# The first norm of a two-block transformer kernel: sums of squares and scales moved from VectorE to TensorE

## The chip, the core and the metric

The kernel runs on one core of a Trainium2 chip. The metric is the device time of one execution in microseconds (us), and lower is better. The core's engines work side by side and wait for each other on semaphores: TensorE (PE, with its weight loads shown as PEld), VectorE (DVE), ScalarE (ACT), GpSimd (POOL) and SyncE (SP), which here issues DMA transfers.

## The reference, cut to what matters

Two networks of two layers run one behind the other on 512 tokens of width 1024. The change touches only the head of the first layer of the first one:

```
cond = silu(c)                                   # 1024 numbers
mod  = cond @ ada_w[0] + ada_b[0]                # 6 x 1024: sh1, sc1, g1, sh2, sc2, g2
h    = x * rsqrt(mean(x*x) + EPS) * (1 + sc1) + sh1
q, k, v, g = split(h @ w_in)                     # retention: four heads of 256
q, k = rotary(q, pos), rotary(k, pos)            # products with cos and sin of an angle
...
```

So the first projection needs x, its mean square for each token, and the 1024 scales and shifts that come out of two matrix-vector products with 1024x1024 pieces of `ada_w`.

## The kernel before

**Layout.** x lies transposed, as eight tiles `xs.x[k]` of 128 channels x 512 tokens. Every fp32 matrix product is made of three matmuls of 128x512 on halves in fp32r: h is split into `hh` and `hl`, a weight tile `raw` into `whi` (ACT, L290) and `wlo` (DVE or POOL, L291), and `mm3` (L296 to L298) issues high by high, high by low and low by high into one PSUM bank `mm`. `load_w` loads a weight tile of 128x1024 through a ring of three `raw` buffers on SP's queue. Engines take their instructions in program order, and a scheduler with priorities (`tc.high_priority`) writes that order when the kernel is built, so an instruction stands behind whatever was put ahead of it on its engine.

**The first norm.** ACT squares the eight tiles of x (L374). DVE adds the squares into `acc` (L376). Then PE multiplies the four 128-column pieces of `acc` by a column of 1/1024 (`sums`, L343): four fp32 matmuls, which the trace shows as eight passes (x8). DVE makes the inverse root in some ten instructions on 128x4 (L322 to L337), and PE spreads it over the partitions with four transposing matmuls (L351).

**The modulation.** `ada_tile` multiplies a tile of `ada_w` (`araw`, three buffers) by `cond`, held alike on all partitions, and sums along the row on DVE (L583, traced as a long and a short instruction), which gives 128 of the 6144 numbers; a tiny addition of the bias follows (L587 or L589). For the first norm 16 tiles are needed, eight scales and eight shifts, in the order scale 0, shift 0, scale 1, ... The other tiles come later, loaded by POOL.

**The normed tiles.** `mod_steps` with the order "late" makes x·R on DVE for two tiles and on POOL for six. ACT applies scale and shift (L421) and rounds to `hh` (L422). POOL subtracts for `hl` (L426). Other norms of the kernel take another branch: `t = x·scale·R` on DVE (L431), `hh = t + shift` on ACT (L433), `hl = t + shift - hh` on DVE (L434).

**Behind it.** `retention` begins with the rotary angle: one integer tile is turned into `cosT` and `sinT` by eight single DVE instructions and three on ACT (L745 to L757). Its first projection makes q and k of head 0 in four PSUM banks (`proj` with four weight tiles). DVE multiplies the four banks by `cosT` and `sinT` (L763 to L766), which frees them. The value projection follows, and then the first score matmul, `mm<-q,q`.

Of the kernel before, what the change touches and what calls it, by code (L numbers as in the profile page):

```python
# [13 lines left out]
F32 = mybir.dt.float32  # L14
# [3 lines left out]
ALU = mybir.AluOpType  # L18
# [84 lines left out]
def _host(i):  # L103
    f32 = np.float32
    h = {}
    h["xT"] = i["x"][0].T.reshape(KT, P, L)
    h["ctxT"] = i["ctx_2"][0].T.reshape(KT, P, LC)
    h["pos"] = np.broadcast_to(i["pos"], (P, L))
    for n, a in (("c1", i["c"]), ("c2", i["c_2"]), ("cc", i["c_ctx_2"])):
# [76 lines left out]
def net_kernel(ctx: ExitStack, tc: tile.TileContext, a: dict, out: bass.AP, dbg=None, stop_at=None):  # L186
# [22 lines left out]
    def tmp(w=L):  # L209
        return tp.tile([P, L], F32, tag="t", name=nm("t"), bufs=TBUFS)[:, :w]  # L210
# [70 lines left out]

    def load_w(src, n=1024):
        wp, _, bufs = next(W["raw"])
# [3 lines left out]
        lo = wp.tile([P, 1024], F32R, tag="wlo", name=nm("wlo"))  # L287
        with tc.high_priority(offset=AHEAD):
            nc.sync.dma_start(raw[:, :n], src)
            S.copy(hi[:, :n], raw[:, :n])  # L290
            next(W["low"]).tensor_tensor(lo[:, :n], raw[:, :n], hi[:, :n].bitcast(F32), ALU.subtract)  # L291
# [14 lines left out]
    def proj(srcs, h, n):  # L306


        w = [load_w(s) for s in srcs]
        p = [mm_ps()[:, :n] for _ in srcs]  # L310
# [93 lines left out]
    def mod_steps(st, R, sc, sh, res, order=None, ext=None):  # L404
# [3 lines left out]
        for k in range(KT):  # L408
            hi, lo = htile(st, k)
            if order == "late":  # L410

                if k == 0:
                    ts = [tmp(n) for _ in range(3)]
                    V.tensor_mul(ts[0], st.x[0], R)
                    V.tensor_mul(ts[1], st.x[1], R)
                    Rs = tmp(n)
                    S.copy(Rs, R)
                    G.tensor_tensor(ts[2], st.x[2], Rs, ALU.mult)
                    yield
                t = ts[k]  # L420
                S.activation(t, t, AF.Identity, bias=sh[:, k:k + 1], scale=sc[:, k:k + 1])  # L421
                S.copy(hi, t)  # L422
                if k + 3 < KT:
                    ts.append(tmp(n))
                    G.tensor_tensor(ts[k + 3], st.x[k + 3], Rs, ALU.mult)
                G.tensor_tensor(lo, t, hi.bitcast(F32), ALU.subtract)  # L426
                res.append((hi, lo))
                yield
                continue
            t = tmp(n)  # L430
# [308 lines left out]

    def retention(st, h, g1, hook, then):  # L740
        with pool("ret") as rp:
# [42 lines left out]

            p = proj(qsrc(0, 0) + qsrc(0, 1), h, L)
            qq, kk_ = rotated(0, p[:2]), rotated(1, p[2:])
# [922 lines left out]
    with ExitStack() as blk:  # L1709
# [3 lines left out]
        open_ada(adas)  # L1713
        first = [t for k in range(8) for t in (8 + k, k)]
        plan = ada_plan([(0, ["1"], first + list(range(16, 48))), (1, ["1"], range(48))])
        hs = {}
        ns = norm_steps(xs, mv("1", 0, 1), mv("1", 0, 0), hs, "late")
        with tc.high_priority(offset=2000):
            for k in range(KT):
                nc.sync.dma_start(xs.x[k], a["xT"][k])  # L1720
            take(ns, 1)
            cond("1", "c1")
            nc.sync.dma_start(pk, a["pack"])
            take(plan, 1)
            take(ns, 1)
            take(plan, 1)
            take(ns, 1)
        for k in range(1, KT):
            with tc.high_priority(offset=500) if k < 3 else nullcontext():
                take(plan, 2)  # L1730
            take(ns, 1)
        take(ns, 9)
        h = hs["x"]
        mid0 = HalfNorm(xs, mv("1", 0, 4), mv("1", 0, 3))
# [8 lines left out]

        retention(xs, h, mv("1", 0, 2), hook_r, mid0)
        if dump("x_mix0"):
# [104 lines left out]
```

## Time and profile before

| | us |
|---|---|
| three runs: median (lowest to highest) | 2926.98 (2925.31 to 2928.30) |
| the profiled execution: its time | 2927.78 |
| the profiled execution: its span in the trace | 2925.9 |
| PE busy in that span | 2833.4 |
| PE busy in 86.20 to 130.00 (43.80) | 43.75 |
| first projection matmul starts | 23.08 |
| first score matmul starts | 86.20 |

The trace is that of the profiled execution; its times count from the start of the span. Its own time is 0.80 us above the median. The granted TensorE clock is given as a share of 2.4 GHz, so 0.50 is the lower of its two levels, 1.2 GHz. In the first 41 us the column shows 1.00 while the spacing of the matmuls is that of the lower level: no clock event is recorded before the first change.

### The profile page before, as it was taken

How to read it: one execution, taken by the hardware profiler on the slowest of the kernel's cores; microseconds unless marked ns; L12 is line 12 of the kernel's file. 1: busy time of each engine (PE TensorE's matmuls, PEld its weight loads, DVE VectorE, ACT ScalarE, POOL GpSimd, SP SyncE). 2: the span in 40 equal slices, each digit the busy share in tenths (PEclk: the TensorE clock that was granted, in tenths of full speed). 3: DMA queues.
4: the chain of work that ended last, by engine and by line, in shares of the span. 5: the costliest groups of instructions: out<-in, count | busy, mean ns of one | idle time of the engine just before them, and what ended most of it. 6: DMA issues, size and time to landing. Idle time of an engine off the chain costs nothing.

```text
span 2925.9 us, 40551 instructions
## 1 busy us (share of the span) xinstructions
PE 2833.4 (97%) x15700; PEld 2382.5 (81%) x15700; DVE 1938.6 (66%) x3558; ACT 1141.8 (39%) x1865; POOL 622.6 (21%) x590
## 2 busy tenths in 40 slices
PE   5999999999998999999999999999999999999999
PEld 3888888878886887888788888888887777788887
DVE  8767667986877668898736678554348467653333
ACT  4433344323753443223434431312237477542331
POOL 4000003443323113332002022221101233022220
PEclk9999999999999999999999999999999999999999
DMA  7445433665655435555212246331214322232232
GB/s 268 136 155 168 158 119 109 221 219 171 219 197 198 150 96 179 174 179 161 76 60 98 72 125 214 112 126 51 70 54 151 100 73 74 65 101 94 91 103 73
DMA packets 122608, 384.77 MB, mean 132 GB/s; under 512 B 13232, under 2 KB 27184, under 8 KB 121392
## 3 DMA queue, kind: packets, MB, share of 16 engines
q1 hardware_dynamic: 97072, 289.90, 30.5%
q0 software_dynamic: 25344, 92.29, 9.9%
q8 instruction: 123, 2.02, 0.3%
q14 instruction: 69, 0.57, 0.1%
HBM read 359.06 MB, written 23.07 MB: 131 GB/s over the span
## 4 chain that ended last, share of the span: by engine, by line
PE 55%; DVE 9%; ACT 2%; issue 1%; POOL 0%; ACTq 0%; DVEq 0%; POOLq 0%
PE mm L296 17%; PE mm L297 17%; PE mm L298 17%; DVE aout L583 1%; DVE wlo L291 1%; DVE al L280 1%; DVE araw L583 1%; PE aux L1637 1%; PE mm L1604 1%; PE mm L1624 1%; DVE t L618 1%; ACT whi L290 1%; PE mm L1432 0%; DVE hl L434 0%; ACT ah L279 0%
## 5 line engine op out<-in xcount | busy, mean ns | idle before, releaser
L296 PE MATMUL mm<-hh,whi 128*128 128x512 f32 (+1 forms) x2872 | 1039.5, 365 | 12.9 <-ACT whi L290 6.2
L297 PE MATMUL mm<-hl,whi 128*128 128x512 f32 (+1 forms) x2872 | 1033.0, 360 | 16.0 <-POOL hl L426 13.6
L298 PE MATMUL mm<-hh,wlo 128*128 128x512 f32 (+1 forms) x2872 | 1031.9, 360 | 0.9 <-DVE wlo L291 0.8
L290 ACT CAST whi<-raw 128x1024 fp32r<-128x1024 f32 (+3 forms) x448 | 447.1, 1002 | 857.4 <-PE mm L297 722.1
L297 PEld LDWEIGHTS mm<-hl,whi 128*128 128x128 f32 x2872 | 545.0, 190 | 98.9 <-POOL hl L426 15.7
L296 PEld LDWEIGHTS mm<-hh,whi 128*128 128x128 f32 x2872 | 542.5, 190 | 101.7 <-issue 7.8
L298 PEld LDWEIGHTS mm<-hh,wlo 128*128 128x128 f32 x2872 | 544.8, 190 | 81.8 <-DVE wlo L291 1.6
L291 DVE TENSOR_TENSOR wlo<-raw,whi 128x1024 fp32r<-128x1024 f32 (+4 forms) x316 | 374.0, 1186 | 216.5 <-ACT whi L290 200.6
L291 POOL TENSOR_TENSOR wlo<-raw,whi 128x1024 fp32r<-128x1024 f32 (+3 forms) x132 | 309.4, 2345 | 915.3 <-ACT whi L290 771.5
L297 PE MATMUL mm<-al,whi 128*128 128x512 f32 (+1 forms) x898 | 330.1, 368 | 3.5 <-DVE al L280 3.5
L296 PE MATMUL mm<-ah,whi 128*128 128x512 f32 (+1 forms) x898 | 329.4, 367 | 2.6 <-ACT ah L279 2.6
L298 PE MATMUL mm<-ah,wlo 128*128 128x512 f32 (+1 forms) x898 | 328.9, 366 | 0.0
L583 DVE CUSTOM_DVE_ANT_0 araw<-araw,cond 128x1024 f32<-128x1024 f32 x192 | 249.0, 1298 | 12.2 <-DMA araw<-in_ada 11.8
L618 DVE SCALAR_TENSOR_TENSOR t<-mm,pk,t 128x511 f32<-128x511 f32 (+5 forms) x286 | 161.0, 581 | 134.9 <-ACT t L620 131.5
L579 POOL DMA_DIRECT2D araw<-in_ada x176 | 96.0, 546 | 658.6 <-DVE mod L583 264.2
L297 PEld LDWEIGHTS mm<-al,whi 128*128 128x128 f32 x898 | 170.6, 190 | 31.2 <-DVE al L280 4.6
L296 PEld LDWEIGHTS mm<-ah,whi 128*128 128x128 f32 x898 | 170.6, 190 | 30.4 <-ACT ah L279 3.0
L298 PEld LDWEIGHTS mm<-ah,wlo 128*128 128x128 f32 x898 | 170.5, 190 | 27.4
L710 DVE SCALAR_TENSOR_TENSOR x<-mm,mod,x 128x512 f32<-128x512 f32 (+1 forms) x115 | 84.2, 733 | 141.4 <-PE mm L298 141.3
L642 ACT ACTIVATE t<-t 128x512 f32<-128x512 f32 x110 | 64.6, 588 | 268.5 <-DVE t L618 250.0
L643 DVE TENSOR_TENSOR t<-mm,t 128x512 f32<-128x512 f32 x110 | 69.9, 636 | 149.8 <-PE mm L298 111.4
L280 DVE TENSOR_TENSOR al<-t,ah 128x512 fp32r<-128x512 f32 x110 | 121.7, 1107 | 41.5 <-ACT ah L279 41.3
(360 smaller groups left out, 3442.4 us busy)
## 6 DMA issues: line engine op xcount, KB each, us to landing
araw<-in_ada POOLq DMA_DIRECT2D x176, 512.0 KB, 4.2
raw<-in_up SPq DMA_DIRECT2D x176, 512.0 KB, 3.6
raw<-in_dn SPq DMA_DIRECT2D x32, 448.0 KB, 3.3
raw<-in_dn SPq DMA_DIRECT2D x32, 384.0 KB, 3.1
raw<-in_qk SPq DMA_DIRECT2D x24, 512.0 KB, 3.6
raw<-in_dn SPq DMA_DIRECT2D x32, 320.0 KB, 2.9
araw<-in_ada SPq DMA_DIRECT2D x16, 512.0 KB, 4.5
raw<-in_rqk SPq DMA_DIRECT2D x16, 512.0 KB, 4.5
```

Of the source, the lines that this page charges most:

```text
L280: eng.tensor_tensor(lo, full, hi.bitcast(F32), ALU.subtract)
L290: S.copy(hi[:, :n], raw[:, :n])
L291: next(W["low"]).tensor_tensor(lo[:, :n], raw[:, :n], hi[:, :n].bitcast(F32), ALU.subtract)
L296: T.matmul(o, lhsT=lh[0], rhs=rh[0], start=first, stop=False)
L297: T.matmul(o, lhsT=lh[0], rhs=rh[1], start=False, stop=False)
L298: T.matmul(o, lhsT=lh[1], rhs=rh[0], start=False, stop=last)
L579: (nc.sync if l == 0 and f < 16 else G).dma_start(raw, a[f"ada{l}"][f])
L583: tc.keep_in_program_order(V.tensor_tensor_reduce(out=o, in0=raw, in1=A[c], scale=1.0, scalar=0.0, op0=ALU.mult, op1=ALU.add, accum_out=m))
L618: V.scalar_tensor_tensor(to, fr, cw[q], to, ALU.mult, ALU.add)
L642: S.activation(t, t, AF.Silu)
L643: V.tensor_mul(t, pv, t)
L710: V.scalar_tensor_tensor(xv, p, gates[st.tag][:, f:f + 1], xv, ALU.mult, ALU.add)
```

## The change

**Squares.** ACT squares each tile of x into a tile of its own. PE multiplies every one of the 32 pieces of 128x128 by the column `inv` and accumulates over the eight tiles in PSUM (L1712). The seven additions on DVE and `sums` are gone here.

**Scales.** A transposed copy of the scale part of `ada_w` (`adas`) is a new input. For each k, `scale(k)` loads 128x1024 of it into one of five buffers `aw` of a pool of their own and PE multiplies its eight pieces by the columns of `cT` (c as 128x8, through ACT's Silu) into one column of the bank `pa` (L1719). One tiny DVE instruction adds 1 and the bias (L1720). The shifts stay with `ada_tile` on DVE.

**Normed tiles.** The "late" branch is deleted, and the first norm goes the way of the others: DVE, ACT, DVE (after: L413, L415, L416). ACT, which before changed its function table for Silu, loads it first.

**Loads.** SP's queue now runs: c1T, the eight tiles of x, `pack`, `aw` 0, cond, `araw` 0, two weight tiles, `aw` 1, `araw` 1, two weight tiles, then `aw` and `araw` by turns. The fourth weight tile waits for a `raw` buffer that the low half of the first one frees. The four weight tiles are handed to `retention` as `w0`.

```diff
-    def load_w(src, n=1024):
+    def load_w(src, n=1024, ahead=AHEAD):
...
-        with tc.high_priority(offset=AHEAD):
+        with tc.high_priority(offset=ahead) if ahead else nullcontext():
...
-        w = [load_w(s) for s in srcs]
+        w = [s if isinstance(s, tuple) else load_w(s) for s in srcs]
...
-            if order == "late":
...
-                t = ts[k]
-                S.activation(t, t, AF.Identity, bias=sh[:, k:k + 1], scale=sc[:, k:k + 1])
-                S.copy(hi, t)
-                if k + 3 < KT:
-                    ts.append(tmp(n))
-                    G.tensor_tensor(ts[k + 3], st.x[k + 3], Rs, ALU.mult)
-                G.tensor_tensor(lo, t, hi.bitcast(F32), ALU.subtract)
...
-            p = proj(qsrc(0, 0) + qsrc(0, 1), h, L)
+            p = proj(w0, h, L)
...
-        first = [t for k in range(8) for t in (8 + k, k)]
-        plan = ada_plan([(0, ["1"], first + list(range(16, 48))), (1, ["1"], range(48))])
+        plan = ada_plan([(0, ["1"], range(16, 48)), (1, ["1"], range(48))])
...
+            cT = small(8)
+            nc.sync.dma_start(cT, a["c1T"])
             for k in range(KT):
                 nc.sync.dma_start(xs.x[k], a["xT"][k])
-            take(ns, 1)
+            nc.sync.dma_start(pk, a["pack"])
+            S.activation(cT, cT, AF.Silu)
+            p = aux_ps()
+            for k in range(KT):
+                sq = tmp()
+                S.activation(sq, xs.x[k], AF.Square)
+                for tb in range(4):
+                    T.matmul(p[:, tb:tb + 1], lhsT=sq[:, tb * P:(tb + 1) * P], rhs=inv[:, 0:1], start=k == 0 and tb == 0, stop=k == KT - 1 and tb == 3)
+            pa = mm_ps()
+
+            def scale(k):
+                aw = stp.tile([P, D], F32, tag="aw", name=nm("aw"), bufs=5)
+                nc.sync.dma_start(aw, a["adas"][k])
+                for kk in range(KT):
+                    T.matmul(pa[:, k:k + 1], lhsT=aw[:, kk * P:(kk + 1) * P], rhs=cT[:, kk:kk + 1], start=kk == 0, stop=kk == KT - 1)
+                V.scalar_tensor_tensor(mods["1", 0][:, 8 + k:9 + k], pa[:, k:k + 1], 1.0, par("adab0", 8 + k), ALU.add, ALU.add)
+
+            scale(0)
             cond("1", "c1")
...
+            ada_tile(0, ["1"], 0)
+            with tc.high_priority(offset=60):
+                R = spread(rsqrt_s(p[:, :4], 4), 4)
+            res, w0 = [], []
+            steps = mod_steps(xs, R, mv("1", 0, 1), mv("1", 0, 0), res)
+            for k in range(KT):
+                if k:
+                    scale(k)
+                    ada_tile(0, ["1"], k)
+                if k < 2:
+                    w0 += [load_w(a["rqk"][8 * k + i], ahead=0) for i in range(2)]
+                take(steps, 1)
```

What the scheduler makes of it on two engines follows; a number behind a tile's name tells one buffer from the next.

On PE, these are the first rows of the program before: the four matmuls of the sum, the spread, and the first two normed tiles against the first weight tile.

```order
L343 MATMUL aux_170<-inv,acc_139 128x1 x4
L351 MATMUL aux_193<-ident,sm_177 128x128 x4
L296 MATMUL mm_355<-hh_198,whi_332 128x512
L297 MATMUL mm_355<-hl_199,whi_332 128x512
L298 MATMUL mm_355<-hh_198,wlo_333 128x512
L296 MATMUL mm_355<-hh_229,whi_332 128x512
L297 MATMUL mm_355<-hl_230,whi_332 128x512
L298 MATMUL mm_355<-hh_229,wlo_333 128x512
```

After, the head of the same queue, from the last of the eight groups of sums on (`t_189` is the last square, `aux_228` the spread root, `mm_195` the bank of the scales, `mm_430` and `mm_431` the first two banks of the projection):

```order
L1712 MATMUL aux_146<-inv,t_189 128x1 x4
L353 MATMUL aux_228<-ident,sm_216 128x128 x4
L1719 MATMUL mm_195<-sm_134,aw_196 128x1 x8
L298 MATMUL mm_430<-hh_245,whi_234 128x512
L299 MATMUL mm_430<-hl_246,whi_234 128x512
L300 MATMUL mm_430<-hh_245,wlo_235 128x512
L298 MATMUL mm_431<-hh_245,whi_240 128x512
L1719 MATMUL mm_195<-sm_134,aw_251 128x1 x8
L299 MATMUL mm_431<-hl_246,whi_240 128x512
L300 MATMUL mm_431<-hh_245,wlo_241 128x512
L298 MATMUL mm_430<-hh_278,whi_234 128x512
```

The one scale group that a step needs now stands between the projection's matmuls, behind the normed tile before it.

On DVE, this is a stretch in the middle of the first norm before: angle steps on `cosT` and `t_317` stand between the reductions of the modulation.

```order
L750 TENSOR_SCALAR cosT<-cosT 128x512
L587 TENSOR_TENSOR mod_74<-mod_74,pk 128x1
L752 SCALAR_TENSOR_TENSOR t_317<-cosT,t_317 128x512
L583 ISA araw_266,mod_74<-araw_266,cond_162 128x1024
L583 ISA mod_74 128x1
L752 SCALAR_TENSOR_TENSOR t_317<-cosT,t_317 128x512
L589 SCALAR_TENSOR_TENSOR mod_74<-mod_74,pk 128x1
L583 ISA araw_270,mod_74<-araw_270,cond_162 128x1024
L583 ISA mod_74 128x1
L752 SCALAR_TENSOR_TENSOR t_317<-cosT,t_317 128x512
```

After, the reduction of the last shift (`araw_400`) and what follows it at the end of the norm (`t_416` is the angle, `hl_405` the last low half of h, `wlo_574` and `wlo_608` low halves of value weights, `araw_602` a tile of the gate `g1`):

```order
L565 ISA araw_400,mod_74<-araw_400,cond_207 128x1024
L565 ISA mod_74 128x1
L569 TENSOR_TENSOR mod_74<-mod_74,pk 128x1
L728 CAST t_416<-t_414 128x512
L293 TENSOR_TENSOR wlo_574<-raw_572,whi_573 128x1024
L416 SCALAR_TENSOR_TENSOR hl_405<-t_406,mod_74,hh_404 128x512
L729 TENSOR_SCALAR t_416<-t_416,pk 128x512
L565 ISA araw_602,mod_74<-araw_602,cond_207 128x1024
L565 ISA mod_74 128x1
L732 TENSOR_SCALAR cosT<-t_416 128x512
L293 TENSOR_TENSOR wlo_608<-raw_606,whi_607 128x1024
L733 TENSOR_SCALAR cosT<-cosT 128x512
```

And a few rows further down, to the first two rotation products, which read the projection's first bank:

```order
L293 TENSOR_TENSOR wlo_794<-raw_792,whi_793 128x1024
L736 TENSOR_SCALAR t_416<-t_416 128x512
L569 TENSOR_TENSOR mod_74<-mod_74,pk 128x1
L565 ISA araw_670,mod_74<-araw_670,cond_207 128x1024
L565 ISA mod_74 128x1
L565 ISA araw_704,mod_74<-araw_704,cond_207 128x1024
L565 ISA mod_74 128x1
L746 TENSOR_TENSOR t_530<-mm_430,cosT 128x512
L747 TENSOR_TENSOR t_532<-mm_430,sinT 128x512
```

The eight angle instructions moved from between the first reductions to behind the last one, where they share the queue with five low halves of weights and four reductions of the next part; the rotation products stand behind all of them, as they stood behind them before.

## Rows read from the trace of the kernel before

**Rows 1.** The page of before: its span and the engines' busy time.

```profile
span 2925.9 us, 40551 instructions
PE 2833.4 (97%) x15700; PEld 2382.5 (81%) x15700; DVE 1938.6 (66%) x3558; ACT 1141.8 (39%) x1865; POOL 622.6 (21%) x590
```

**Rows 2.** Windows: start:end, length, busy of PE, PEld, DVE, ACT, POOL, PEclk, DMA, GB/s.

```profile
0.00:37.70 37.70, 5.37 (x16) 3.62 (x16) 27.40 (x43) 17.27 (x22) 18.44 (x20) 1.00 0.75 268
...
41.00:45.00 4.00, 4.00 (x19) 3.29 (x18) 3.93 (x10) 1.44 (x2) 1.50 (x1) 1.00 0.73 226
...
64.00:86.20 22.20, 21.97 (x96) 17.70 (x96) 21.61 (x37) 11.87 (x18) 2.15 (x4) 1.00 0.52 175
86.20:130.00 43.80, 43.75 (x220) 37.27 (x219) 26.80 (x51) 17.92 (x32) 1.06 (x2) 1.00 0.43 140
```

**Rows 3.** Timeline of PE and PEld, 0 to 40 us: start, busy time, instruction.

```profile
12.01 1.78 PEld L343 LDWEIGHTS aux<-inv,acc 128*128 128x128 f32 x8 [12.01 <-issue]
12.04 1.84 PE L343 MATMUL aux<-inv,acc 128*128 128x1 f32 x8 [12.04 <-DVE acc L376]
...
16.00 1.09 PE L351 MATMUL aux<-ident,sm 128*128 128x128 f32 x4 [2.13 <-DVE sm L335]
23.08 0.80 PE L296 MATMUL mm<-hh,whi 128*128 128x512 f32 x1 [5.98 <-ACT whi L290]
...
37.72 0.80 PE L297 MATMUL mm<-hl,whi 128*128 128x512 f32 x1 [5.04 <-POOL hl L426]
...
39.17 0.63 PE L297 MATMUL mm<-hl,whi 128*128 128x512 f32 x1
39.60 0.63 PE L298 MATMUL mm<-hh,wlo 128*128 128x512 f32 x1
```

**Rows 4.** Timeline of DVE, 0 to 43 us.

```profile
13.92 0.16 DVE L322 TENSOR_SCALAR sm<-aux 128x4 f32<-128x4 f32 x1 [2.02 <-PE aux L343]
...
15.82 1.22 DVE L583 CUSTOM_DVE_ANT_0 araw<-araw,cond 128x1024 f32<-128x1024 f32 x1
...
42.30 0.42 DVE L745 CAST t<-t 128x512 f32<-128x512 int32 x1
```

**Rows 5.** Lines by form: count, ns min/median/max, first and last start, shapes.

```profile
L431 DVE SCALAR_TENSOR_TENSOR t<-x,mod,aux x16: 725/739/747, 1643.5 to 2258.8; 128x512 f32<-128x512 f32 x16
L433 ACT ACTIVATE hh<-t,mod x24: 702/725/1323, 1456.3 to 2259.6; 128x512 fp32r<-128x512 f32 x24
```

**Rows 6.** Lines by form, 0 to 80 us: the two halves of a weight tile.

```profile
L290 ACT CAST whi<-raw x11: 1028/1046/1054, 22.0 to 75.6; 128x1024 fp32r<-128x1024 f32 x11
L291 DVE TENSOR_TENSOR wlo<-raw,whi x9: 1211/1216/2207, 24.2 to 77.6; 128x1024 fp32r<-128x1024 f32 x9
```

**Rows 7.** Timeline of SP and ACT; a DMA issue with KB and us to landing.

```profile
0.74 3.71 SPq L1720 DMA_DIRECT2D x<-in_xT  x8
...
3.56 0.63 ACT L374 ACTIVATE acc<-x 128x512 f32<-128x512 f32 x1 [1.54 <-DMA x<-in_xT]
...
6.56 3.90 ACT L374 ACTIVATE t<-x 128x512 f32<-128x512 f32 x6 [1.60 <-DMA x<-in_xT]
...
raw<-in_rqk SPq DMA_DIRECT2D x4, 512.0 KB, 6.4
```

**Rows 8.** Timeline of PE at the next sum of squares.

```profile
108.64 0.95 PE L343 MATMUL aux<-inv,acc 128*128 128x1 f32 x8
```

**Rows 9.** Timeline of PE at the first score matmul.

```profile
85.97 0.39 PE L298 MATMUL mm<-whi,hl 128*128 128x512 f32 x1
86.20 0.39 PE L296 MATMUL mm<-q,q 128*128 128x512 f32 x1
```

**Rows 10.** Windows of three later stretches, columns as in group 2.

```profile
450.55:453.96 3.41, 1.76 (x13) 1.59 (x13) 2.81 (x7) 0.90 (x3) 0.00 (x0) 1.00 0.55 162
453.96:457.37 3.41, 3.15 (x15) 2.72 (x14) 3.41 (x17) 2.00 (x5) 0.00 (x0) 0.50 0.60 195
884.04:887.45 3.41, 3.41 (x14) 3.22 (x15) 0.87 (x1) 0.00 (x0) 1.19 (x2) 0.50 0.39 115
```

More of the change, by code (lines that the diff above doesn't have):

```diff
@@ L107, in _host @@
     h["ctxT"] = i["ctx_2"][0].T.reshape(KT, P, LC)
+    h["c1T"] = i["c"].reshape(KT, P).T
+    h["adas"] = _wt(i["ada_w"][0][:, D:2 * D])
     h["pos"] = np.broadcast_to(i["pos"], (P, L))
@@ L409, in mod_steps @@
             hi, lo = htile(st, k)
-            if order == "late":
[L412 to L419, printed above, removed]
-                t = ts[k]
-                S.activation(t, t, AF.Identity, bias=sh[:, k:k + 1], scale=sc[:, k:k + 1])
-                S.copy(hi, t)
-                if k + 3 < KT:
-                    ts.append(tmp(n))
-                    G.tensor_tensor(ts[k + 3], st.x[k + 3], Rs, ALU.mult)
-                G.tensor_tensor(lo, t, hi.bitcast(F32), ALU.subtract)
-                res.append((hi, lo))
-                yield
-                continue
             t = tmp(n)
@@ L737, in ffn, with retention @@
                 j0 += nk
-    def retention(st, h, g1, hook, then):
+    def retention(st, h, w0, g1, hook, then):
         with pool("ret") as rp:
@@ L1713, in net_kernel @@
         open_ada(adas)
-        first = [t for k in range(8) for t in (8 + k, k)]
-        plan = ada_plan([(0, ["1"], first + list(range(16, 48))), (1, ["1"], range(48))])
+        plan = ada_plan([(0, ["1"], range(16, 48)), (1, ["1"], range(48))])
         hs = {}
-        ns = norm_steps(xs, mv("1", 0, 1), mv("1", 0, 0), hs, "late")
-        with tc.high_priority(offset=2000):
+        with pool("start") as stp:
+            cT = small(8)
+            nc.sync.dma_start(cT, a["c1T"])
             for k in range(KT):
@@ L1720, in net_kernel @@
                 nc.sync.dma_start(xs.x[k], a["xT"][k])
-            take(ns, 1)
-            cond("1", "c1")
[L1723 to L1733, printed above, removed]
+            nc.sync.dma_start(pk, a["pack"])
@@ L1734, in net_kernel @@
+            h = res
         mid0 = HalfNorm(xs, mv("1", 0, 4), mv("1", 0, 3))
@@ L1742, in hook_r @@
                     s5_params()
-        retention(xs, h, mv("1", 0, 2), hook_r, mid0)
+        retention(xs, h, w0, mv("1", 0, 2), hook_r, mid0)
         if dump("x_mix0"):
```

## The prediction, made before the changed kernel ran

> **What bounds the kernel now.** I read the page first: PE is busy for 97% of the span [rows 1], so the end moves when PE's queue moves. Then the windows, stage by stage. Up to 37.70 us PE is busy for 5.37 us only, while DVE has 27.40; from 86.20 to 130.00 it is busy for 43.75 of 43.80 [rows 2]. So the head of the kernel is where PE waits, and from the first score matmul, which starts at 86.20 [rows 9], it waits for almost nothing. The two programs give PE the same instructions in the same order from that matmul on. I therefore take its start as a milestone: what it moves by, the end moves by.
>
> The timelines show what the head waits for. PE's sum of squares starts at 12.04, when DVE has added the last square, and the spread of the root ends at 16.00 + 1.09 = 17.09. The first projection matmul starts at 23.08, and PE runs without gaps from 37.72, when POOL delivers the second low half [rows 3]. Of 192 matmuls of 128x512 ahead of the milestone 188 lie behind 37.72, and they fill the 48.5 us up to it nearly without a break: 21.97 of 22.20 us are busy from 64.00 [rows 2]. The clock is at its lower level at first: two matmuls start 39.60 - 39.17 = 0.43 us apart [rows 3]; from 41 on 19 fit into 4.00 us [rows 2], and at the milestone the spacing is 86.20 - 85.97 = 0.23 us [rows 9].
>
> **Unit prices.** A one-column pass on PE at the lower level: eight take 1.84 us [rows 3]. A matmul of 0.63 is followed by the next after 0.43, so 0.20 of each last one is drain, and a pass costs (1.84 - 0.20) / 8 = 0.205. At the higher level eight take 0.95 [rows 8], with a drain of 0.39 - 0.23 = 0.16 [rows 9]: 0.10 a pass. A group of eight matmuls 128x1 in fp32 is 16 passes, since four gave x8: 16 x 0.205 + 0.2 = 3.5 us at the lower level, 1.75 at the higher. What sets the pass is its weight load: PEld needs 1.78 for eight [rows 3], 0.22 each. The Trainium skill (TensorE: Matmul & The Clock Gate, section LDWEIGHTS) puts a load at columns / 1.2 ns, so 107 ns for 128 columns; by that the 64 passes of the squares would be done in 6.9 us instead of 13.1, under the arrival of x. The row measures twice that on the same shape at this level, and I go by the row.
>
> DVE: a product of t or low half of h 0.74, ACT's high half 0.73 [rows 5]; a weight's high half 1.05, its low half 1.22 [rows 6]; a shift's reduction 1.22, a tiny instruction 0.16, a step with one operand 0.42 [rows 4]. These are the durations without POOL beside it; the low half also shows 2.21 [rows 6], the upper bound for the long ones.
>
> **The change, step by step.**
>
> *Squares.* SP issues one load more ahead of x, 3.71 / 8 = 0.46 us; the first square then starts at 3.56 + 0.46 = 4.02 and ends at 4.65, the last ends at 6.56 + 3.90 + 0.46 = 10.92 [rows 7]. PE needs 64 passes: 4.75 + 64 x 0.205 + 0.2 = 18.1. The seven additions on DVE go, but PE now ends the sum, 4.2 us later than before (12.04 + 1.84 = 13.88 [rows 3]). The root and the spread are unchanged, 17.09 - 13.88 = 3.2: 21.3.
>
> *First scale.* It stands behind the spread on PE: 21.3 + 3.5 = 24.8. Its tile was issued about 5 us into the span and needs some 6 to land (6.4 for a weight of the same size [rows 7]), so it is there. Then, one behind the other, the tiny DVE instruction 0.16, t 0.74, on DVE the shift's reduction with its two tiny ones 1.22 + 0.32, and the high half 0.73: 3.2, so 28.0. ACT rounds the first weight behind that, 1.05: the first projection matmul starts at about 29 (before 23.08). The low half of this weight is ready at about 30.3.
>
> *Second scale.* It stands behind four projection matmuls, 31 to 34.6, and the same 3.2 follow: dense work from about 38, as before (37.72). What POOL's low halves cost before, two groups on PE and the later sum cost now.
>
> *Scales in the dense stretch.* Before, PE met nothing but projection matmuls here. Now six more groups stand among them. Eleven matmuls at 0.43 lead to 42.7, with the clock up by then as before; scale 2 ends at 44.8, seven matmuls and scale 3 later it is 48.1. Each further step holds one group 1.75, twelve matmuls 12 x 0.23 = 2.76 and a wait: the low half of this step comes on DVE behind the tiny one and the next t, 0.16 + 0.74 + 0.74 + 0.1 for the handover = 1.75 after the group's end, and only six matmuls, 1.36, stand between. So 0.4 is open, and a step is 4.9. Four of them: scale 7 ends at 67.7.
>
> *The end of the norm on DVE.* The rotation products, which free the bank that the third value bank needs, stand behind all of this on DVE: five low halves of weights (6.1), five reductions (6.1), six products (4.4), five steps with one operand (2.1), two rotation products (about 1.4 by the price of t): 20.1 us from the end of scale 7, so 87.8. PE itself, with 72 matmuls (16.5) from 67.7, would be there at 84.2, so it idles for 3.6 us. Before, the angle was being worked out from 42.30 [rows 4], under POOL's slow start; that cover is gone.
>
> *Sum.* From 87.8 there are 48 matmuls to the milestone, 11.0: 98.8 instead of 86.20, +12.6. On the profiled execution's 2927.78 that is 2940.4; this execution is 0.8 above the median of 2926.98, so **2940**.
>
> *What I price at nothing.* SP: its queue stands at the fourth weight tile until the first low half is done at 30.3, and the scales 2 to 7 wait behind. That weight lands at about 37; at the 268 GB/s of the first stretch [rows 2] each further 512 KB takes 2 us, a scale with its shift 4, against 4.9 us a step. Scale 2 would be there at 39, needed at 42.7. The cover is 4 us; if the rate were a third lower, each later step would lose about 1 us, 5 in all. One load of ACT's function table less: under the loads of x. POOL: it has nothing in the norm now, and nobody waits for it.
>
> **The rivals.**
>
> *The clock stays or falls low in the norm.* Each step has a group of one-column passes and a wait. After a stretch with PE busy 1.76 of 3.41 us the clock was at 0.50 in the next [rows 10]. At the lower level a step costs 1.75 + 12 x 0.2 - 0.4 = 3.8 more. One or two such steps give 2944 to 2948, all to the end of the norm 2955 or so. Against it: from 64.00 to 130.00 the level held at 1.00 [rows 2].
>
> *The clock comes up in the squares.* PE is now busy without a break from 4.75 on. If the clock rose some 4 us in, as it did behind 37.72, 45 of the passes would cost 0.10, and the sum ends at 13.2 (-4.9). Two groups of 1.75 (-3.5) and the first eleven matmuls at 0.23 (-2.2) follow: +12.6 - 10.6 = +2, so 2929, no change that this kernel's measurement can tell (0.2%, 5.9 us, either way). The Trainium skill (TensorE: Matmul & The Clock Gate, Part 1) says that sustained matmul activity releases the clock, and by that page this is what would happen. Against it speaks 884.04 to 887.45: PE is busy there for all of 3.41 us, and the clock is 0.50 [rows 10]. So a busy PE has been seen at the lower level.
>
> *Faster.* It takes the clock of the last case and an end of the norm in which DVE is not late: -3.6 more is 2926, still no change. To pass 2921 the dense stretch must begin before 26 and lose nothing behind: PE's own work from there is 188 x 0.23 + 6 x 1.75 = 53.7, so a milestone below 80. It decides at the sum of squares, which would have to end near the last square, 10.9.
>
> **Chances and range.** The forecast 0.58, on its own 2934 to 2947: DVE's long instructions at 2.21 would add 5, loads 5, and the late low halves may cost less (up to -6 if DVE is ready with PE and the steps have no wait). Clock low 0.20. Clock up early 0.16, of which a part falls between. Faster 0.06. The range 2928 to 2952 leaves out the faster case and the worst of the low clock. Slower 0.78, same 0.16, faster 0.06.
>
> **What would show it.** L1712 as a row of about 64 passes that ends near 18, not 11; the first projection matmul near 29 and the gapless stretch from 38; the groups of L1719 at 3.5 and later 1.75 us; the last shift's reduction near 69 and a wait of PE for DVE's rotation products (releaser t, from the first bank) just ahead of the milestone, which starts near 99; equal spacing behind it. I am wrong if passes in the squares run at 0.10, if scale 2 waits for a DMA, or if the milestone moves and the end doesn't.

## The result: 0.5% slower, and the profile after

The changed kernel takes 2941.56 us (median of five, 2940.41 to 2950.56) against 2927.20 (2925.31 to 2930.08). The ratio is 1.0052 with an interval of 1.0040 to 1.0064. The prediction was 2940. The profiled execution took 2941.22, 13.4 more than that of before.

The span on the page of the kernel after, beside [rows 1]:

```profile
span 2939.4 us, 40867 instructions
```

TensorE's timeline after, up to the third scale, beside [rows 3]:

```profile
4.99 13.79 PE L1712 MATMUL aux<-inv,t 128*128 128x1 f32 x64 [4.99 <-ACT t L1710]
20.91 1.08 PE L353 MATMUL aux<-ident,sm 128*128 128x128 f32 x4 [2.13 <-DVE sm L337]
21.79 3.41 PE L1719 MATMUL mm<-sm,aw 128*128 128x1 f32 x16
29.26 0.80 PE L298 MATMUL mm<-hh,whi 128*128 128x512 f32 x1 [4.06 <-ACT whi L292]
...
31.54 3.41 PE L1719 MATMUL mm<-sm,aw 128*128 128x1 f32 x16
...
38.07 1.22 PE L298 MATMUL mm<-hh,whi 128*128 128x512 f32 x2 [2.06 <-ACT hh L415]
...
42.42 1.84 PE L1719 MATMUL mm<-sm,aw 128*128 128x1 f32 x16
```

The first row is the squares: 64 passes in 13.79 us, from the first square on; they end at 18.78, not 13.88. The first scale ends at 25.20, the second stands among matmuls at 31.54, gapless work begins at 38.07. At 42.42 the third group takes 1.84 us, so the clock has risen by then.

And further on, to the first score matmul (beside [rows 9]):

```profile
65.96 1.84 PE L1719 MATMUL mm<-sm,aw 128*128 128x1 f32 x16
...
84.82 0.39 PE L300 MATMUL mm<-whi,hl 128*128 128x512 f32 x1
87.40 0.50 PE L298 MATMUL mm<-whi,hh 128*128 128x512 f32 x1 [2.19 <-DVE t L747]
...
98.41 0.39 PE L298 MATMUL mm<-q,q 128*128 128x512 f32 x1
```

The last scale's group ends at 67.80. The row of 87.40 shows a wait of 2.19 us for VectorE's second rotation product. The milestone is at 98.41, 12.2 later than before.

VectorE's timeline at the end of the norm:

```profile
67.84 0.16 DVE L1720 SCALAR_TENSOR_TENSOR mod<-mm,pk 128x1 f32<-128x1 f32 x1 [2.09 <-PE mm L1719]
...
70.70 0.42 DVE L728 CAST t<-t 128x512 f32<-128x512 int32 x1
...
82.23 1.23 DVE L293 TENSOR_TENSOR wlo<-raw,whi 128x1024 fp32r<-128x1024 f32 x1 [0.55 <-ACT whi L292]
...
86.06 0.69 DVE L746 TENSOR_TENSOR t<-mm,cosT 128x512 f32<-128x512 f32 x1
86.67 0.68 DVE L747 TENSOR_TENSOR t<-mm,sinT 128x512 f32<-128x512 f32 x1
```

Between the last scale (67.84) and the product that frees the bank (86.67) it has one gap only, of 0.55 us for ScalarE's high half of a weight. The rest is reductions, low halves and, from 70.70 on, the angle.

The waits of TensorE in 0 to 100 us, after (engine and line that waited, who released it, total, times, longest):

```profile
PE aux L1712 <- ACT t L1710: 5.0, 1, 5.0
PE mm L298 <- ACT whi L292: 4.1, 1, 4.1
PE mm L298 <- DVE t L747: 2.2, 1, 2.2
PE aux L353 <- DVE sm L337: 2.1, 1, 2.1
PE mm L298 <- ACT hh L415: 2.1, 1, 2.1
PE mm L299 <- DVE hl L416: 1.4, 5, 0.7
```

No load of a scale is among them, and nothing waits for GpSimd any more.

The next sum of squares starts 12.2 us later too (120.79, before 108.64 [rows 8]). Further on the shift changes, for the most part where one of the two kernels has a stretch at the lower clock and the other has none. From the sum at 463.48 (before 452.82) to that at 2220.18 (before 2209.64) it is 10.5 to 11.1 us: in 443.00 to 449.00 the kernel before was granted 0.72, and the changed one in 455.00 to 461.00 the full 1.00. At the last sum it is 12.2 again: in 2272.00 to 2280.00 the changed kernel was granted 0.79, and the kernel before in 2261.00 to 2269.00 the full 1.00. The last 1.3 of the 13.5 by which the spans differ arise right behind that sum. TensorE waits 2.56 us for it in both kernels. Before, with the window behind it:

```profile
2564.71 0.58 PE L343 MATMUL aux<-inv,acc 128*128 128x1 f32 x4 [2.56 <-DVE acc L511]
```

```profile
2565.00:2575.00 10.00, 9.37 (x73) 8.65 (x73) 8.81 (x24) 3.06 (x6) 0.00 (x0) 1.00 0.36 105
```

And after:

```profile
2576.92 0.58 PE L345 MATMUL aux<-inv,acc 128*128 128x1 f32 x4 [2.56 <-DVE acc L493]
```

```profile
2577.20:2587.20 10.00, 9.40 (x62) 8.86 (x62) 7.52 (x21) 2.60 (x6) 0.00 (x0) 0.83 0.33 107
```

The granted clock fell behind this wait in one kernel and not in the other. So the 13.5 are the 12.2 of the head and a balance of later differences, most of them single stretches at the lower clock.

### The profile page after: what moved, and what is told of

Same layout as the page of the kernel before. It is cut to its first block, busy times and chain, and to the rows that moved or that the text cites. A ratio compares the mean times of both kernels' runs of the same rounds, so it can differ in the third digit from the quotient of the medians.

```text
span 2939.4 us, 40867 instructions
## 1 busy us (share of the span) xinstructions
PE 2865.3 (97%) x15884; PEld 2414.4 (82%) x15884; DVE 1924.2 (65%) x3549; ACT 1134.7 (39%) x1856; POOL 596.2 (20%) x576
## 4 chain that ended last, share of the span: by engine, by line
PE 55%; DVE 9%; ACT 2%; issue 1%; POOL 0%; ACTq 0%; DVEq 0%; POOLq 0%
PE mm L298 17%; PE mm L299 17%; PE mm L300 17%; DVE aout L565 1%; DVE wlo L293 1%; DVE al L282 1%; DVE araw L565 1%; PE mm L1587 1%; PE aux L1620 1%; PE mm L1607 1%; DVE t L600 1%; ACT whi L292 1%; PE mm L1415 0%; ACT t L1596 0%; DVE hl L416 0%
## 5 line engine op out<-in xcount | busy, mean ns | idle before, releaser
L565 DVE CUSTOM_DVE_ANT_0 araw<-araw,cond 128x1024 f32<-128x1024 f32 x184 | 238.3, 1297 | 7.6 <-DMA araw<-in_ada 7.2
L692 DVE SCALAR_TENSOR_TENSOR x<-mm,mod,x 128x512 f32<-128x512 f32 (+1 forms) x115 | 84.2, 733 | 140.4 <-PE mm L300 140.4
```

What stands on the lines that cost most here:

```text
L565: tc.keep_in_program_order(V.tensor_tensor_reduce(out=o, in0=raw, in1=A[c], scale=1.0, scalar=0.0, op0=ALU.mult, op1=ALU.add, accum_out=m))
L692: V.scalar_tensor_tensor(xv, p, gates[st.tag][:, f:f + 1], xv, ALU.mult, ALU.add)
```

## The experiments

The theory was that of the prediction: TensorE's one-column passes stand in the path (squares, scales), and at the end of the norm VectorE is late. The rivals were that the squares lie under the loads, that VectorE sets the pace in any case, that late loads do it, and that the clock decides. All comparisons are ratios to the kernel before on the same chip; its median was 2928.2 to 2929.8 on those chips.

| run | first score matmul, us | ratio to before | interval |
|---|---|---|---|
| before | 86.20 | 1 | |
| after | 98.41 | 1.0052 | 1.0040 to 1.0064 |
| e1_sums_vector | 96.69 | 1.0022 | 1.0012 to 1.0033 |
| e2_scale1_early | 95.89 | 1.0036 | 1.0022 to 1.0051 |
| e3_angle_early | 91.57 | 1.0014 | 1.0005 to 1.0024 |
| e4_warm | 105.56 | 1.0057 | 1.0042 to 1.0072 |
| e5_scales_vector | 86.1 | 1.0002 | 0.9992 to 1.0011 |
| e6_own_buffer | 103.1 | 1.0053 | 1.0037 to 1.0068 |
| e7_head | 91.7 | 1.0023 | 1.0014 to 1.0033 |
| e8_hybrid | 82.7 | 1.0001 | 0.9991 to 1.0010 |
| e9_both_vector | 82.1 | 0.9986 | 0.9977 to 0.9996 |
| e10_low_half_later | 81.0 | 0.9980 | 0.9972 to 0.9989 |
| e11_scale_ring | 79.6 | 0.9976 | 0.9967 to 0.9984 |
| e12_ring_and_weight | 79.7 | 0.9977 | 0.9968 to 0.9986 |

### The squares back on VectorE

```diff
-            p = aux_ps()
-            for k in range(KT):
-                sq = tmp()
-                S.activation(sq, xs.x[k], AF.Square)
...
+            p = sums([Squares(xs).all()], 4, 0)
```

> Only the sums of squares go back to VectorE (seven additions, then eight passes on TensorE). Theory (the 64 one-column passes at the lower clock level set the end of the sum, and the head is a chain of handovers that nothing else covers): the sum ends near 14.3 us instead of 18.8, the first projection matmul starts near 23.3 instead of 29.3, and everything behind follows: the first score matmul near 92.4 instead of 98.4, the time some 6 us under the changed kernel, about 2935. Rival (the loads of the scales and weights would come just as late, so that the squares are hidden behind them): the first projection matmul stays above 27 and the time moves by under 2 us.

TensorE's timeline of this run:

```profile
12.25 1.84 PE L345 MATMUL aux<-inv,acc 128*128 128x1 f32 x8 [12.25 <-DVE inv L1486]
...
22.86 0.80 PE L298 MATMUL mm<-hh,whi 128*128 128x512 f32 x1 [3.86 <-ACT whi L292]
...
31.67 1.22 PE L298 MATMUL mm<-hh,whi 128*128 128x512 f32 x2 [2.06 <-ACT hh L415]
...
46.35 3.40 PE L1714 MATMUL mm<-sm,aw 128*128 128x1 f32 x16
```

The head does as the theory says: the first projection matmul comes 6.4 us sooner (22.86 for 29.26), the gapless stretch too (31.67 for 38.07). But the milestone moves by 1.7 only. The row of 46.35 shows why: a group of scales takes 3.40 us there, as at the lower level. The windows say it outright (columns as in [rows 2]):

```profile
43.50:47.00 3.50, 3.24 (x10) 2.66 (x11) 1.51 (x4) 0.72 (x1) 0.00 (x0) 0.56 0.72 263
47.00:50.50 3.50, 3.50 (x15) 3.40 (x16) 0.67 (x2) 0.00 (x0) 0.00 (x0) 0.50 0.56 219
50.50:54.00 3.50, 3.50 (x9) 2.66 (x9) 2.20 (x5) 0.72 (x1) 0.00 (x0) 0.50 0.16 20
```

The clock was at its lower level for nearly all of these three windows in the middle of the norm. This profile is of the slowest of eight executions (2940.05; the fastest took 2932.02). Over the executions the ratio falls from 1.0052 to 1.0022, some 9 us with an uncertainty of nearly 5. That fits the 6 us, and not a change of under 2. With the first projection matmul at 22.86, the rival (above 27, under 2 us) is out.

### The second scale straight behind the first

```diff
             ada_tile(0, ["1"], 0)
+            scale(1)
...
-                if k:
+                if k >= 2:
                     scale(k)
```

> The second scale's eight matmuls are issued straight behind the first scale's, into TensorE's idle 4 us before the first projection matmul, instead of between projection matmuls; nothing else changes. Theory (the group at 31.5 to 34.8 and the wait of 2.1 us behind it are on the path): the gapless stretch starts at 31 to 33 instead of 38. Then the third scale's load shows, since it stands on the queue behind the fourth weight tile, which is held until about 30.5: scale 2 starts at 37.5 to 38 instead of 42.4, so the first score matmul comes near 94 and the time near 2937. Rival (the chain on VectorE behind the first norm tile sets the pace whatever TensorE does): scale 2 starts at 41 or later and the time stays within 2 us of the changed kernel.

The third scale starts at 37.00 instead of 42.42, and no wait is for a load, although the theory expected the third one's load to show. Fourteen projection matmuls stand ahead of this group and not seventeen, so that 0.7 of these 5.4 us is no gain, and 4.7 is. At the milestone 2.5 arrive. TensorE's timeline and a window of it:

```profile
37.00 1.84 PE L1719 MATMUL mm<-sm,aw 128*128 128x1 f32 x16
...
83.22 0.50 PE L298 MATMUL mm<-whi,hh 128*128 128x512 f32 x1 [2.78 <-DVE t L747]
```

```profile
84.00:87.00 3.00, 3.00 (x9) 2.28 (x8) 3.00 (x6) 1.22 (x2) 0.00 (x0) 0.52 0.66 229
```

VectorE is late by 2.78 instead of 2.19 us, since TensorE is sooner: 0.6 of the gain. Behind that wait the clock is at 0.52 for three microseconds, and from the end of the wait to the milestone it takes 12.67 us (95.89 - 83.22) instead of 11.01 (98.41 - 87.40). Here the wait cost 1.7 more than its own length. What is left of the 4.7 is the 2.5.

### The angle during VectorE's wait for the first scale

```diff
+            with tc.issue_after(chain["end"]):
+                turned = angle(pos_i)
+            scale(0, lambda: tc.issue_after(turned))
...
+            with tc.issue_after(turned):
+                ada_tile(0, ["1"], 0)
```

> The eight angle steps are done on VectorE while it waits for the first scale (20.8 to 25.2 us), with the positions loaded behind the first scale's tile; only sine and cosine on ScalarE stay behind the norm. Theory (VectorE's end of the norm is late by 2.2 us, TensorE would be ready): the wait of 2.19 us for the rotation products is gone, the first score matmul comes at 95.5 to 96.5 instead of 98.4, the time near 2939, and no more than that, since TensorE itself comes next. Rival (the angle steps lie in VectorE's shadow and the wait is for something else, the low halves or the gate's reductions): the wait stays above 1.5 us and the first score matmul within 0.7 us of 98.4.

TensorE's timeline from the second scale to the milestone:

```profile
28.05 0.80 PE L298 MATMUL mm<-hh,whi 128*128 128x512 f32 x1 [2.94 <-ACT hh L415]
28.64 3.41 PE L1721 MATMUL mm<-sm,aw 128*128 128x1 f32 x16
...
37.06 1.84 PE L1721 MATMUL mm<-sm,aw 128*128 128x1 f32 x16
...
91.57 0.39 PE L298 MATMUL mm<-q,q 128*128 128x512 f32 x1
```

The wait for the rotation products is gone, but the gain, 6.8 us, is nearly three times what the theory allowed. The edit also moved the second scale: it stands behind one projection matmul here (28.64) and not behind four. The clean comparison is with the run before this one, whose third scale starts at the same time behind as many matmuls (37.00 and 37.06): from there on the early angle is worth 95.89 - 91.57 = 4.3 us. That is the wait of 2.78 and the 1.7 that the stretch at the lower clock behind it cost there. Against the changed kernel the 6.8 are the 4.7 of the second scale, as in the run before, and the 2.19 of the wait. So the theory's size for the angle holds.

### TensorE kept busy ahead of the squares

```diff
+            with tc.high_priority(offset=4000):
+                for _ in range(8):
+                    T.matmul(pa, lhsT=ones[:, :P], rhs=ones, start=True, stop=True)
```

> Eight matmuls of 128x512 in fp32 on a tile of ones, which nothing reads as a result, run on TensorE ahead of the squares (1.2 to some 8 us). Theory (the passes of the squares and of the first two scales are dear because TensorE is at its lower level, and it would hold the higher one through them once it has it): the 64 passes take some 6.5 us instead of 13.8 and end near 14.5, scales 0 and 1 take 1.8 instead of 3.4 each, the first score matmul comes at 88 to 93 and the time at 2931 to 2936. Rival (one-column passes do not hold the higher level, or the idle time behind the sum loses it again): passes at 0.21 us for most of the squares, a sum that ends at 18 or later, scales at 3.4, and a time within 2 us of the changed kernel or above it.

TensorE's timeline, and its windows:

```profile
11.44 3.07 PE L1718 MATMUL aux<-inv,t 128*128 128x1 f32 x27
14.38 8.03 PE L1718 MATMUL aux<-inv,t 128*128 128x1 f32 x37
22.27 3.55 PE L1723 MATMUL mm<-sm,aw 128*128 128x1 f32 x16
```

```profile
11.40:13.00 1.60, 1.60 (x16) 1.55 (x14) 0.08 (x1) 0.00 (x0) 0.00 (x0) 1.00 1.02 417
13.00:15.00 2.00, 2.00 (x17) 2.00 (x17) 0.00 (x0) 1.06 (x1) 0.00 (x0) 0.85 1.03 422
15.00:17.00 2.00, 2.00 (x11) 2.00 (x11) 0.00 (x0) 0.00 (x0) 0.00 (x0) 0.50 1.03 420
```

The clock did rise: the first 27 passes of the squares take 3.07 us, 0.11 each. But at 13 to 15 us it falls, with TensorE busy for all of the 2.00 us, and the other 37 passes take 8.03 us, 0.21 each; the first scale again takes 3.55 us. So the rival holds: here 64 one-column passes without a gap did not keep the higher level, which eight matmuls of the same number type with 512 columns had brought. Those take until 11.44 and not until some 8, so that the squares end at 22.4. The first score matmul is later than in the changed kernel (105.56). The times do not tell the two apart (1.0057 and 1.0052, with intervals that overlap).

### The scales back on VectorE, and both back

```diff
             def scale(k):
-                aw = stp.tile([P, D], F32, tag="aw", name=nm("aw"), bufs=5)
-                nc.sync.dma_start(aw, a["adas"][k])
-                for kk in range(KT):
...
+                ada_tile(0, ["1"], 8 + k)
```

> The eight scales go back to VectorE (two reductions a step, tiles in the order scale, shift); the squares stay on TensorE and the normed tiles keep their new way. Theory (eight groups of one-column passes on TensorE, 3.4 us each at the lower level and 1.8 at the higher, stand in the path, and VectorE has room for the reductions: it was idle for 2.1 us of every 5.0 us step): a step becomes VectorE's, two reductions, t, low half, 4.4 us instead of 5.0, and the first two scales no longer stand between matmuls. Norm done on VectorE near 61, rotation products near 78, first score matmul 88 to 90 instead of 98.4, the time some 9 us under the changed kernel. Rival (VectorE becomes the bound as it was before the change, so that moving the scales off it is what helps): first score matmul at 97 or later.

The milestone is at 86.1, better than either theory. The ratio is 1.0002: the whole loss is gone with the squares still on TensorE. VectorE does set the pace now (TensorE waits 14.1 us in all for high halves, and ScalarE, which makes them, waits for VectorE's shifts), but that pace is the faster one.

The second run has this edit and that of the first experiment.

> Squares and scales both on VectorE as before the change; what stays of the change is the normed tiles' way (VectorE, ScalarE, VectorE, nothing on GpSimd), the order of the loads and the weights loaded inside the loop. Theory (the loss is in the two moves to TensorE, and the rest of the change is a gain, since GpSimd's products and low halves held TensorE until 37.7 us): first projection matmul near 21, first score matmul near 84, thus 2 us before that of the kernel before (86.2) and 14 before that of the changed one; the time 0 to 3 us under the kernel before. Rival (the new way of the normed tiles loads VectorE with t and the low halves, and it cannot carry the reductions as well): first score matmul at 90 or later, slower than before.

TensorE's waits in 0 to 100 us, of this run:

```profile
PE mm L298 <- ACT hh L415: 12.9, 7, 3.2
...
PE mm L298 <- DVE t L747: 1.1, 1, 1.1
```

And the longest of the kernel before:

```profile
PE mm L297 <- POOL hl L426: 13.6, 4, 7.2
```

With 82.1 and a ratio of 0.9986 (0.9977 to 0.9996) this is slightly faster than the kernel before. So the part of the change that is in neither move is a gain of 4.1 us at the milestone. The largest piece of it is likely that GpSimd no longer makes products and low halves, for which TensorE waited 13.6 us before; that piece was not tried alone, nor was the new order of the loads. The two moves to TensorE together cost 98.41 - 82.1 = 16.3 at the milestone, and by the ratios some 19 us with an uncertainty of 4 to 5.

### Three repairs with the scales on TensorE, and half of the scales

The first has the edits of the first two experiments, and the angle steps issued from the third tile on; in the second the scales 4 to 7 are reductions.

> The scales stay on TensorE; three repairs of the changed kernel together: squares summed on VectorE, the second scale straight behind the first one, the angle steps spread over the steps from the third tile on with the positions loaded early. Theory (the three losses add up: 6 at the squares, 5 at the second scale, 2 to 5 at the end of the norm): the gapless stretch starts near 25, the first score matmul at 83 to 86, with no wait for the rotation products; the time 12 to 15 us under the changed kernel and about that of the kernel before. Rival (the second of the clock's levels is lost in the steps, or loads come too late for a head that starts 13 us sooner): first score matmul at 90 or later, with rows at 0.43 us spacing behind 40 us or a wait for a load of a scale.

> As the one with three repairs, but the scales 4 to 7 on VectorE (reductions) and only 0 to 3 on TensorE. Theory (from the third step on a group of passes costs TensorE 1.75 us, while VectorE has 2 us to spare in each step): TensorE saves four groups, 7 us, the first score matmul comes at 77 to 81, 5 to 9 us before that of the kernel before, and the time 5 to 9 us under it. Rival (VectorE's two reductions a step with t, low half and the low halves of the value weights make it the bound): first score matmul within 2 us of the one with the scales on TensorE, with a wait of TensorE for low halves of h or for the rotation products.

Timeline and window of the first of the two:

```profile
23.20 0.80 PE L298 MATMUL mm<-hh,whi 128*128 128x512 f32 x1 [0.66 <-ACT whi L292]
...
40.41 3.40 PE L1716 MATMUL mm<-sm,aw 128*128 128x1 f32 x16
...
47.23 3.41 PE L1716 MATMUL mm<-sm,aw 128*128 128x1 f32 x16
```

```profile
40.00:60.00 20.00, 20.00 (x79) 17.63 (x78) 9.04 (x20) 2.69 (x4) 0.70 (x1) 0.58 0.60 219
```

The head starts 6 us sooner than after, as in the first experiment, and no wait for the rotation products is left. But the first of the two rivals decides, the loss of the higher clock level: from 40 to 60 us the mean granted clock is 0.58, two groups of scales take 3.4 us each, and the milestone is 91.7. One of the ten executions took 2926.18 and the others 2933 to 2938. With half of the scales on VectorE the milestone is 82.7, short of 77 to 81: TensorE waits 5.9 us for high halves, so VectorE is the bound there, and from 37.40 to 41.00 the granted clock was 0.53. That is no better than with all of them there (82.1, the run before). Over the executions it is worse: the ratios, on the same chip, are 1.0001 and 0.9986.

### A buffer of its own for the fourth weight

```diff
-                    w0 += [load_w(a["rqk"][8 * k + i], ahead=0) for i in range(2)]
+                    w0 += [load_w(a["rqk"][8 * k + i], ahead=0, raw=stp.tile([P, D], F32, tag="raw3", name="raw3") if k and i else None) for i in range(2)]
```

> The changed kernel, with a buffer of its own for the fourth weight tile, so that the load queue is not held until the first low half is done (10.8 to 30.9 us) and the scales 2 to 7 are issued 18 us sooner. Theory (that hold was priced at nothing, since no scale's load ends a wait of TensorE): the third scale's group starts at 42.4 and the first score matmul at 98.4 as in the changed kernel, each within 0.5 us; the time within 2 us of the changed kernel's. Rival (late loads stretch the steps): the third scale's group starts before 41 and the first score matmul at 96 or sooner.

The queue is no longer held at the fourth weight: the third scale's load is issued at 13.4 us instead of 30.9. The third group starts at 43.54, not sooner but 1.1 later; 0.6 of that stands at the first square already (5.62 for 4.99), and the rest is a clock that rises a few matmuls later (the group takes 2.06 us, not 1.84). The ratio, 1.0053, is that of the changed kernel. So the loads were rightly priced at nothing, though both starts lie outside the half microsecond that was expected. That the milestone is at 103.1 is likely not the buffer: TensorE's clock was at 0.60 in 50 to 54 us, and again down behind its wait of 2.3 us for the rotation products (0.72 in 90 to 94 us).

### Going on from the faster version

The low half of each tile behind the next scale's reduction, then the scales' tiles through five buffers of their own, then the fourth weight's buffer as well. The edits of the first two:

```diff
-                take(steps, 1)
+                hi, lo = htile(xs, k)
+                t = tmp()
...
+                if last:
+                    low(*last)
+                last = (k, t, hi, lo)
```

```diff
-                ada_tile(0, ["1"], 8 + k)
+                aw = stp.tile([P, D], F32, tag="aw", name=nm("aw"), bufs=5)
+                nc.sync.dma_start(aw, a["ada0"][8 + k])
...
```

> Squares and scales on VectorE as in the run with both undone; the low half of each normed tile is issued behind the next scale's reduction, so that VectorE does not wait for ScalarE's high half. Theory (VectorE sets the pace of that version, with a step of 4.75 us of which 0.79 is this wait): a step of 4.0 us, the norm's end on VectorE near 54.5 instead of 58.9, the first score matmul at 77.5 to 80 instead of 82.1, the time some 3 us under that version and 6 to 8 under the kernel before. Rival (two tiles of reductions and a weight tile for each step of 4 us are 1.5 MB, near the rate of 400 GB/s that the loads reach, so that the loads take over): waits of VectorE for the reductions' tiles of 0.5 us and more in each step, first score matmul at 81 or later.

> As the run with the low half later, but the scales' tiles come through five buffers of their own (those that the changed kernel gives to its transposed tiles), the shifts' through the three as before. Theory (VectorE's waits of 4.3 us for tiles are for a free buffer, not for the rate: in that run 40 to 60 us moved 303 GB/s only): the waits for tiles fall under 1 us, the norm's end on VectorE comes near 54 instead of 57.9, the first score matmul at 76 to 79 instead of 81.0, the time 2 to 5 us under that run. Rival (the rate of some 400 GB/s sets the pace): waits as long, first score matmul within 1 us of 81.

> As the one before, and the fourth weight tile has a buffer of its own, so that the load queue is not held behind the first low half. Theory (with the tiles of five buffers the hold of the queue is what is left, and it ends about when the tiles of the third step are needed, so little shows): first score matmul within 1 us of the run with the five buffers. Rival (the hold delays the tiles of the third and fourth step): a wait of 1 us or more for them in the run before that is gone here, first score matmul 1 to 3 us sooner.

VectorE's waits from 16 to 70 us, first with the low half later, then with the five buffers:

```profile
DVE araw L565 <- DMA araw<-in_ada: 4.3, 4, 1.8
```

```profile
DVE t L728 <- DMA t<-in_pos: 3.0, 1, 3.0
```

The first edit turned the wait for ScalarE into one for loads, 4.3 us, which is the rival's effect, and the milestone, 81.0, is where the rival put it (part of that is a fall of the clock behind a wait of TensorE of 2.45 us); the second showed that it was for buffers and not for the rate, since it is gone. What is left is a wait for the positions that the rotary angle needs. The milestone is 79.6, somewhat short of 76 to 79. The fourth weight's buffer changes nothing here either (79.7). The best ratio is 0.9976, 7 us under the kernel before; the three intervals overlap.

## Why the prediction was right

**The squares.** Priced to end at 18.1, they end at 18.78. Counted as there, without the drain of 0.2, a pass was (13.79 - 0.2) / 64 = 0.212 against 0.205. An estimate from the Trainium skill (TensorE: Matmul & The Clock Gate, section LDWEIGHTS) is 0.107 a pass; this trace, with 0.212, contradicts it at the lower level. Undoing it brings the first projection matmul 6.4 us forward.

**The first two scales.** 24.8, 29, 31 and 38 were predicted for the first group's end, the first projection matmul, the second group and the gapless stretch; 25.2, 29.26, 31.54 and 38.07 were measured.

**The scales in the dense stretch.** Group 2 was put at 42.7 to 44.8 and came at 42.42 to 44.26; a step was put at 4.9 and is 5.03 (65.96 - 60.93); scale 7 ends at 67.80 for 67.7. The wait in a step was put at 0.4 and is 0.67 in the first of the four and 0.2 in the others. Here two errors cancel: scale 3 ends 0.4 sooner than predicted, and the four steps take 0.5 longer. (By its own terms the prediction's scale 2 would end at 42.7 + 1.75 = 44.45, not at 44.8, and its faster case at 2929 - 3.6 = 2925.4, not at 2926. Neither changes the forecast.)

**The end of the norm.** The rotation product that frees the bank was put at 87.8 and ends at 87.35. That TensorE would idle for 3.6 us was too much, it is 2.19: it was done at 85.2 and not at 84.2 (74 matmuls stand there and not 72, and a wait of 0.2), and the product came 0.4 sooner. That this wait is on the path is shown by the early angle.

**The sum.** +12.6 was predicted for the milestone and 12.2 measured. The steps are the predicted ones, their ends off by 1.0 us or less and not all in the same direction; that the total is off by 0.4 only is in part luck. The step from there, that the end moves by the same, missed 1.3 us and holds on balance only: behind the milestone the shift went down to 10.5 and up to 13.5 with single stretches at the lower clock, and the prediction named the clock only in the norm. In the fourteen profiles the span less the milestone lies between 2838.2 (e4_warm) and 2842.4 us (e7_head), so differences of one or two microseconds at the end say little about the head.

**The loads and GpSimd, priced at nothing.** The loads: shown by the fourth weight's own buffer. GpSimd: that nobody waits for it any more is likely most of a gain of 4.1 us, which shows when both moves are undone. The sum has it without naming it, since it went by times of its own from the start of the span and not by differences.

**The rivals.** The clock did not come up in the squares: 64 passes at the lower level's price. The Trainium skill (TensorE: Matmul & The Clock Gate, Part 1) says that sustained matmul activity releases the clock; here the squares were without a gap and did not do so, and when other matmuls had brought the clock up, they lost it. That the clock falls low in the norm had 0.20. It did not happen in this profile (1.00 from 40 to 100 us). It did in six of the seven others with scales on TensorE, all but that with the early angle: in the second experiment behind a wait of 2.78 us only, and in the first, in the three repairs, with half of the scales, with the fourth weight's own buffer and with TensorE kept busy also where no wait of more than 0.8 us stands ahead. So it is luck, as far as the runs show, that the profile of the changed kernel has none: the run with the fourth weight's buffer, which differs from it in that buffer alone, has two. With all scales back on VectorE it was 1.00 throughout in two profiles, and it fell in the last three, there only behind waits of 2.4 to 2.8 us for a high or a low half. A window of the changed kernel, the same of the run with both moves undone, and one behind such a wait in the run with five buffers:

```profile
40.00:100.00 60.00, 56.36 (x287) 46.38 (x286) 46.38 (x88) 20.24 (x32) 3.87 (x7) 1.00 0.60 210
```

```profile
40.00:100.00 60.00, 51.11 (x240) 41.33 (x239) 53.02 (x99) 27.17 (x45) 4.39 (x8) 1.00 0.66 214
```

```profile
60.00:64.00 4.00, 4.00 (x12) 3.13 (x11) 4.00 (x5) 1.05 (x1) 0.00 (x0) 0.57 0.76 246
```

So this rival's chance was rather too small. What else makes it fall beside such waits stays open, and so does why a wait of 2.19 us (after, 87.40) and one of 2.56 (before, 2564.71) were not followed by a fall. The changed kernel's executions spread over 10 us where those of before spread over 5; that the clock does it is likely, but no trace of a long one was taken.

## What to carry to other kernels

Work that one engine does in one column per pass is not free because the engine idles at that place: here it stood in a queue with what others waited for, and the sum of squares ended at 18.78 with the 64 passes and at 13.88 with the seven additions that they replaced. An edit that moves load between engines should be taken apart before it is kept or dropped: the loss of 16 us was in the two moves, and a gain of 4 in what came with them. And a wait of TensorE can cost more than its length, by what its clock does behind it (1.7 us more in the run with the second scale early).

## What the runs showed of the hardware

TensorE lost the higher clock while it was busy without a break on 128x1 passes (13.00 to 15.00 us in the run with TensorE kept busy: busy 2.00 of 2.00, granted 0.85, then 0.50). Waits of TensorE of 2.31 to 2.78 us, with matmuls on both sides, were followed by the lower level too, but not all: one of 2.56 us was in the changed kernel (2576.92) and was not in the kernel before (2564.71). A pass of one column takes 0.21 us at the lower level and 0.11 at the higher (37 passes in 8.03 us and 27 in 3.07, in the run with TensorE kept busy).
